# New costs for transposes and a new clock rule in the model that orders a two-layer hybrid encoder

## The chip, the core and the metric

The kernel runs on one core of a Trainium2 chip. The time is the device time of one execution in microseconds. The engines are PE (matmuls; its weight loads are shown as PEld), DVE, ACT and POOL (elementwise work), and SP, which issues DMAs. PE's clock is granted at one of two levels, 1.2 or 2.4 GHz; a granted clock of 1.00 means 2.4 GHz throughout.

## The reference

Two requests (prompt and sample, 1024 tokens of 1024 channels each) go through two layers with shared weights. Cut to what matters:

```
mod = silu(c) @ ada_w + ada_b;  shift, scale, gate = split(mod, 3)
h = rmsnorm(x, norm_pre) * (1 + scale) + shift
u = h @ w_in                  # pool 256 | q 512 | k 128 | v 128 | rg 256 | gate 1024
y = concat(pool_mixer(u_pool), gqa_attention(q, k, v), rglru(u_rg)) * silu(u_gate)
x = x + gate * rmsnorm(y @ w_out, norm_post)
```

The attention has 8 query heads and 2 key/value heads of 64 channels over all 1024 tokens, with normed and rotated q and k. The pool mixer takes centred means with four window lengths. The recurrent branch has a short convolution and a scan in both directions.

## The kernel before

**Slices.** One pair of layer and request is a slice: n = 0 (layer 0, prompt), 1 (layer 0, sample), 2 (layer 1, prompt), 3 (layer 1, sample). Matrix products are made with fp16 operands split in a high and a low part, three matmuls for one. A slice loads x, norms and transposes it (hT), projects and rotates q, k and v, runs the side columns in the order of the list ORDER (recurrent, gate, pool columns), runs 64 attention units, and makes the output projection in 8 tiles of 128 tokens. Slices 0 and 2 also scale and split the weights (wsplit_gen, wo_ahead) and store the split ones for the slices 1 and 3. The second layer's modulation (ada1_gen, weights adaw) is made after the first output projection has begun.

**An attention unit** (L1211 and on) is 128 queries of one head. PE makes 1024 scores in a pair of PSUM banks; DVE takes their maximum (mx); ACT makes the exponential p, then its fp16 part; POOL or DVE subtracts for the low part (both in the tile hh); a transposing DMA (dma_t, L477) turns hh into pT; PE multiplies 24 blocks of pT with v (the PV group).

**The planner.** No loop nest sets the order. Each piece of work is a Python generator with a rank, a *stream*. At each yield it says which engines, tiles, buffers and banks the next step needs. While the program is built, the class Order keeps a simulated time for the engines P, A, D, G (POOL), S (SP's issuing) and X (the transfers), and lets go the stream whose step can go first, and of those that can go now the one with the lowest rank:

```
key = (max(t, self.now), z[0])          # run(): earliest time, then rank
t = max(t, free[e] - tune[e])           # eligible(): look-ahead of engine e
```

The instructions of all engines and SP's queue are written in that order, and engines keep it on the chip. The simulated times come from constants in the helpers (act, tt, mms, dma, dma_t). The clock rule (Order.clock) doubles a matmul's planned time while the simulated PE is not "warm". Some choices, DVE or POOL for a subtraction for example, go to whichever engine the model sees free first (soonest, L481), with a handicap in POOL's favour (slack, hslack, sslack).

**The entries.** TUNE has one dict a slice: ranks of its streams (tab, v, rgt, attn, main, side, w, gate and others; a slice's ranks count from 100 n), look-aheads P, A, D, G, S, X, the number of buffers that are kept free (spare), of score pairs (np) and of output tiles that may be open at once (wopen), the side column from which w_out is loaded (wos), and how side columns are tied to attention units (pace). LAYER has, for a layer, how many modulation weights (fly) and how many pieces of w_out (wfly) may be in flight. These places read the entries that the change touches:

```
wsplit_gen(n, C_K, 256, ("qkv", 0), 100*n + TUNE[n]["q"] if n else START["qw"], keep)   # L1746
sub_any(lo, x, hi, TUNE[0]["hslack"])                                                     # L900
spawn(rank - TUNE[n]["gate"], tail(j, out[0]))                                            # L1372, 1388
cond=lambda: t - left.get("t", 0) < TUNE[n]["wopen"]                                      # L1699
cond=lambda: fly[0] < LAYER[l]["wfly"] and ...                                            # L1586
```

Of the kernel before, what the change touches and what calls it, by code (L numbers as in the profile page):

```python
# [16 lines left out]
P = 128  # L17
D = 1024
# [9 lines left out]


TUNE = [  # L30
    dict(h=-9.8, tab=-61.5, rgw=-62.8, qw=11.3, q=30.3, main=39.6, v=-93.1, rgt=6.2, attn=13.3,
         wprep=16.5, wo=39.7, side=108.5, gate=1.45, ysc=107.7, ysp=100.7, w=68.8, work=8, ds=3, nfly=8,
         s0=4, pace=(4, 61), wos=8, deep=3, f_major=5, spare=0, qkeep=1, wkeep=7, wokeep=0, slack=2.19,
         hslack=1.35, margin=0.33, P=0.6, A=1.22, D=1.01, G=1.25, S=1.3, X=2.5, nb=4, np=2, wopen=3,
         spill=2, sslack=0.0),
    dict(h=-88.0, tab=-138.2, rgw=-45.0, qw=-61.2, q=-181.1, main=65.6, v=-122.9, rgt=21.0, attn=-30.4,
         wprep=107.1, wo=85.3, side=97.8, gate=1.86, ysc=66.7, ysp=108.8, w=79.4, work=8, ds=2, nfly=5,
         s0=0, pace=(14, 64), wos=10, deep=3, f_major=6, spare=2, qkeep=5, wkeep=2, wokeep=9, slack=3.75,
         hslack=3.82, margin=0, P=0.07, A=0.92, D=0.36, G=1.39, S=1.66, X=1.74, nb=4, np=3, wopen=4,
         spill=2, sslack=0.0),  # L40
    dict(h=-56.5, tab=-131.7, rgw=-43.7, qw=-41.0, q=-17.5, main=-3.7, v=-94.1, rgt=51.8, attn=-16.0,
         wprep=71.4, wo=90.7, side=118.4, gate=0.71, ysc=142.5, ysp=110.2, w=62.9, work=6, ds=2, nfly=6,
         s0=3, pace=(15, 38), wos=9, deep=2, f_major=1, spare=4, qkeep=2, wkeep=0, wokeep=1, slack=2.33,
         hslack=2.48, margin=0.36, P=2.36, A=1.02, D=0.83, G=0.625, S=0.35, X=1.72, nb=6, np=2, wopen=4,
         spill=2, sslack=0.0),
    dict(h=-38.8, tab=-7.4, rgw=44.8, qw=-59.1, q=43.0, main=31.5, v=86.0, rgt=62.7, attn=36.1,
         wprep=226.9, wo=-31.1, side=118.1, gate=0.51, ysc=119.3, ysp=81.6, w=59.6, work=10, ds=3, nfly=5,
         s0=5, pace=(0, 64), wos=10, deep=4, f_major=3, spare=1, qkeep=5, wkeep=1, wokeep=0, slack=2.26,
         hslack=2.6, margin=0.87, P=0.28, A=0.14, D=0.45, G=0.9, S=1.99, X=0, nb=4, np=3, wopen=4,
         spill=2, sslack=0.28),  # L50
]
START = dict(x=(6, 16), xr=(-53.8009657012761, 1.4378218455368525), h=11.7, qw=-116.3, qw2=-141.6, qwa=9,
             prt=7, crow=4, prow=2, ada=95.9, keep=0)
LAYER = [
    dict(fly=5, keep=3, wfly=1, wfrom=(0, 0), wrank=15.7, ada=-17.0, akeep=5),
    dict(fly=3, keep=2, wfly=1, wfrom=(1, 1), wrank=163.6, ada=69.7, akeep=8),
]
LAT = {
# [30 lines left out]
class Order:  # L89
# [144 lines left out]
    def clock(self, t):  # L234

        while self.window < int(t / 3.4133):
            self.warm = self.busy / 3.4133 > (0.38 if self.warm else 0.75)
            self.window += 1
            self.busy = 0.0
        return 1.0 if self.warm else 2.0  # L240
# [64 lines left out]
def cols(ap):  # L305
    n = 1
    for x in ap.shape[1:]:
        n *= x
    return n
# [3 lines left out]
def tile_hymba_encoder(  # L313
# [43 lines left out]
    od = Order({"s": NS, "H": 2, "h": NH})  # L357
# [119 lines left out]

    def dma_t(out, in_):
        nc.sync.dma_start_transpose(out=out, in_=in_)
        od.dma(2.3 * cols(in_) / 2048, [out], [in_], 1.7, 0.6)  # L480

    def soonest(*choice):

# [89 lines left out]
    G = {}  # L573
# [522 lines left out]
    def qk_transpose(src, out, key):  # L1096
        yield need("S", [src], s=1)
        t = slot([P, 16, P], F16, "qkT")
        flat = "p a b c d -> p (a b c d)" if len(src.shape) == 5 else "p a b c -> p (a b c)"
        dma_t(t, src.rearrange(flat))  # L1100
        free(src)
        out[key] = t
# [107 lines left out]
    def attn_gen(n, rank):  # L1210
# [3 lines left out]
        def unit(i, S):  # L1214
# [25 lines left out]
            yield need("S", [hh], u=1)  # L1240
            pT = slot([P, 16, P], F16, "pT", "u")
            dma_t(pT, hh.rearrange("p a s -> p (a s)"))
            free(hh)
            if (hp, q) not in O:
# [583 lines left out]
```

## Time and profile before

| what | value |
|---|---|
| median of 3 runs | 1909.93 us (1905.5 to 1915.82) |
| the profiled execution, time | 1907.34 us |
| its span, first to last instruction | 1905.6 us |
| mean granted clock of PE | 0.972 |
| PE busy | 1723.2 us, 90% of the span |
| DVE, ACT, POOL busy | 1292.7, 1136.9, 754.5 us |
| DMA | 323.58 MB, mean 170 GB/s |

Read the table from PE down: what PE does not fill of the span is what an order can change. In the profile, "idle before" is an engine's idle time ahead of a group of instructions, with what ended it, the releaser. L395 is the line of the helper that issues matmuls, so groups are told apart by tiles. Matmul ends are modelled, so a busy PE is not PE at its peak.

### The profile page before, as it was taken

The page shows a single profiled execution, that of the slowest core. Times are in us where ns is not written, and L with a number is a line of the kernel's source. Part 1 is how long each engine was busy: PE and PEld are TensorE (multiplying, and loading weights), DVE is VectorE, ACT ScalarE, POOL GpSimd, SP SyncE. Part 2 cuts the span into 40 slices and gives each one's busy share as a digit, 9 for nine tenths or more (in the row PEclk, how much of TensorE's full clock was granted, in tenths as well). Part 3 has the DMA queues.
Part 4 walks back from the last instruction along what each step waited for, and adds up shares of the span by engine and source line. Part 5 has one row for each costly group of instructions (what it writes and reads, how often), then busy time and mean ns, then how long its engine had stood idle before and what let it go on. Part 6 is the DMA issues. An engine that isn't in the chain of part 4 may idle for free. (4 is left out here: it accounts for less than half of the span.)

```text
span 1905.6 us, 35807 instructions
## 1 busy us (share of the span) xinstructions
PE 1723.2 (90%) x14267; PEld 996.0 (52%) x14267; DVE 1292.7 (68%) x2333; ACT 1136.9 (60%) x1761; POOL 754.5 (40%) x597
## 2 busy tenths in 40 slices
PE   4899898978999888899899999998789999999898
PEld 2564554545455446455456647454445755555543
DVE  4697986776246889677545779867744477867831
ACT  3765766786215666687643277678854256877831
POOL 2722643453321335342524226245553214634423
PEclk9899999998999998999899999999999999999999
DMA  9565799997465667899933365698994322999943
GB/s 342 160 171 166 142 226 236 175 183 232 137 251 166 151 148 133 168 196 217 249 122 122 98 146 112 153 238 163 183 228 171 100 67 37 178 186 195 210 108 130
DMA packets 672592, 323.58 MB, mean 170 GB/s; under 512 B 597880, under 2 KB 628776, under 8 KB 672424
## 3 DMA queue, kind: packets, MB, share of 16 engines
q1 hardware_dynamic: 672424, 321.29, 72.6%
q8 instruction: 111, 1.82, 0.4%
q14 instruction: 57, 0.47, 0.1%
HBM read 128.28 MB, written 46.15 MB: 92 GB/s over the span
## 5 line engine op out<-in xcount | busy, mean ns | idle before, releaser
L423 POOL TENSOR_TENSOR hh<-p,hh 128x1024 f16<-128x1024 f32 x183 | 395.5, 2166 | 425.5 <-ACT hh L410 363.4
L395 PE MATMUL psum<-hT,w 128*128 128x512 f16 x2304 | 538.2, 382 | 8.3 <-ACT w L410 3.4
L459 DVE TENSOR_REDUCE mx<-psum 128x1 f32<-128x1024 f32 x256 | 312.2, 1219 | 128.1 <-PE psum L395 107.1
L395 PEld LDWEIGHTS <-w 128*128 128x128 f16 x2304 | 222.5, 99 | 275.5 <-issue 33.5
L395 PE MATMUL psum<-wo,y 128*128 128x512 f16 x1536 | 345.3, 383 | 4.1 <-DVE y L442 2.3
L395 PE MATMUL psum<-qkT,qkT 128*128 128x512 f16 x1024 | 268.2, 389 | 45.3 <-ACT p L410 26.8
L395 PEld LDWEIGHTS <-pT 128*128 128x128 f16 x6144 | 216.1, 100 | 133.8 <-DMA pT<-hh 96.4
L395 PE MATMUL psum<-v,pT 128*128 128x64 f16 x6144 | 230.3, 196 | 60.7 <-DMA pT<-hh 60.0
L410 ACT ACTIVATE p<-psum,mx,qksc 128x1024 f32<-128x1024 f32 x183 | 219.2, 1199 | 105.0 <-DVE mx L444 60.0
L395 PE MATMUL psum<-w,hT 128*128 128x256 f16 x2304 | 272.1, 275 | 8.6 <-POOL hT L423 8.6
L395 PEld LDWEIGHTS <-hT 128*128 128x128 f16 x2304 | 224.6, 99 | 60.3 <-issue 18.5
L395 PEld LDWEIGHTS <-y 128*128 128x128 f16 x1536 | 150.1, 99 | 179.8 <-issue 7.3
L410 ACT ACTIVATE hh<-p 128x1024 f16<-128x1024 f32 x183 | 192.0, 1053 | 4.0
L395 PEld LDWEIGHTS <-qkT 128*128 128x128 f16 x1024 | 94.7, 100 | 141.9 <-issue 64.0
L410 ACT ACTIVATE junk<-psum 128x512 bf16<-128x512 f32 x64 | 38.3, 598 | 176.5 <-PE psum L395 171.3
L450 DVE SCALAR_TENSOR_TENSOR ot<-psum,ors,gp 128x512 f32<-128x512 f32 x64 | 45.1, 745 | 132.7 <-POOL ors L423 132.7
L423 POOL TENSOR_TENSOR ot<-ot,xres 128x1024 f32<-128x1024 f32 x31 | 72.9, 2352 | 94.0 <-DVE ot L450 58.4
L423 POOL TENSOR_TENSOR ws<-ws,neghalf 128x1 f32<-128x1 f32 x46 | 29.0, 634 | 195.0 <-DVE ws L442 195.0
L423 DVE TENSOR_TENSOR hh<-psum,hh 128x1024 f16<-128x1024 f32 x73 | 89.0, 1219 | 25.2 <-ACT hh L410 24.7
L410 ACT ACTIVATE psum<-psum,mx,qksc 128x1024 f32<-128x1024 f32 x73 | 85.5, 1171 | 28.1 <-DVE mx L444 27.8
L410 ACT ACTIVATE hh<-psum 128x1024 f16<-128x1024 f32 x73 | 74.5, 1020 | 1.7
L410 ACT ACTIVATE gth<-psum,wu 128x512 f32<-128x512 f32 x64 | 43.8, 684 | 44.9 <-PE psum L395 44.9
(212 smaller groups left out, 2100.0 us busy)
## 6 DMA issues: line engine op xcount, KB each, us to landing
adaw<-in_ada_w_dram SPq DMA_DIRECT2D x48, 512.0 KB
wraw<-in_w_in_dram SPq DMA_DIRECT2D x36, 512.0 KB
wd<-w SPq DMA_DIRECT2D x36, 512.0 KB
w<-wd SPq DMA_DIRECT2D x36, 512.0 KB
wo<-wd SPq DMA_DIRECT2D x32, 512.0 KB
woraw<-in_w_out_dram SPq DMA_DIRECT2D x16, 512.0 KB
wd<-wo SPq DMA_DIRECT2D x16, 512.0 KB
xmid<-ot SPq DMA_DIRECT2D x16, 512.0 KB
```

What stands on the lines that cost most here:

```text
L395: nc.tensor.matmul(out[:, :m], lhsT, rhs, start=start and i == 0, stop=stop and i == len(pairs) - 1)
L410: nc.scalar.activation(out=out, in_=in_, func=func, **kw)
L423: eng.tensor_tensor(out=out, in0=a, in1=b, op=op)
L450: nc.vector.scalar_tensor_tensor(out=out, in0=a, scalar=s, in1=b, op0=op0, op1=op1)
L459: nc.vector.tensor_reduce(out=out, in_=a, op=op, **{"axis": AX.X, **kw})
```

## The change

Two constants of dma_t rise: the time that a 2048-column transpose holds the transfer resource, and the time that it holds SP's queue. Both constants of the clock rule change, so that the simulated PE turns warm less readily and stays so a little more readily. Entries of TUNE and LAYER get other values. No instruction is added or removed; the order, and the engine of those operations that have a choice, come out of the planner anew.

```diff
--- before.py
+++ after.py
@@ -28,31 +28,31 @@
 
 
 TUNE = [
-    dict(h=-9.8, tab=-61.5, rgw=-62.8, qw=11.3, q=30.3, main=39.6, v=-93.1, rgt=6.2, attn=13.3,
+    dict(h=-9.8, tab=-61.5, rgw=-62.8, qw=11.3, q=39.5, main=39.6, v=-93.1, rgt=6.2, attn=13.3,
          wprep=16.5, wo=39.7, side=108.5, gate=1.45, ysc=107.7, ysp=100.7, w=68.8, work=8, ds=3, nfly=8,
          s0=4, pace=(4, 61), wos=8, deep=3, f_major=5, spare=0, qkeep=1, wkeep=7, wokeep=0, slack=2.19,
-         hslack=1.35, margin=0.33, P=0.6, A=1.22, D=1.01, G=1.25, S=1.3, X=2.5, nb=4, np=2, wopen=3,
+         hslack=2.0, margin=0.33, P=0.6, A=1.22, D=1.02, G=1.25, S=1.3, X=2.99, nb=4, np=2, wopen=3,
          spill=2, sslack=0.0),
-    dict(h=-88.0, tab=-138.2, rgw=-45.0, qw=-61.2, q=-181.1, main=65.6, v=-122.9, rgt=21.0, attn=-30.4,
+    dict(h=-88.0, tab=-138.2, rgw=-45.0, qw=-61.2, q=-181.1, main=65.6, v=-122.9, rgt=23.6, attn=-14.4,
          wprep=107.1, wo=85.3, side=97.8, gate=1.86, ysc=66.7, ysp=108.8, w=79.4, work=8, ds=2, nfly=5,
-         s0=0, pace=(14, 64), wos=10, deep=3, f_major=6, spare=2, qkeep=5, wkeep=2, wokeep=9, slack=3.75,
-         hslack=3.82, margin=0, P=0.07, A=0.92, D=0.36, G=1.39, S=1.66, X=1.74, nb=4, np=3, wopen=4,
+         s0=0, pace=(14, 64), wos=10, deep=3, f_major=6, spare=1, qkeep=5, wkeep=2, wokeep=9, slack=3.75,
+         hslack=3.82, margin=0, P=0.07, A=1.29, D=0.36, G=1.39, S=1.66, X=1.74, nb=4, np=3, wopen=4,
          spill=2, sslack=0.0),
-    dict(h=-56.5, tab=-131.7, rgw=-43.7, qw=-41.0, q=-17.5, main=-3.7, v=-94.1, rgt=51.8, attn=-16.0,
-         wprep=71.4, wo=90.7, side=118.4, gate=0.71, ysc=142.5, ysp=110.2, w=62.9, work=6, ds=2, nfly=6,
+    dict(h=-56.5, tab=-120.9, rgw=-43.7, qw=-41.0, q=-17.5, main=-3.7, v=-95.2, rgt=51.8, attn=-16.0,
+         wprep=71.4, wo=90.7, side=118.4, gate=0.1, ysc=142.5, ysp=110.2, w=62.9, work=6, ds=2, nfly=6,
          s0=3, pace=(15, 38), wos=9, deep=2, f_major=1, spare=4, qkeep=2, wkeep=0, wokeep=1, slack=2.33,
-         hslack=2.48, margin=0.36, P=2.36, A=1.02, D=0.83, G=0.625, S=0.35, X=1.72, nb=6, np=2, wopen=4,
-         spill=2, sslack=0.0),
+         hslack=2.48, margin=0.36, P=2.36, A=1.02, D=0.83, G=0.625, S=0.35, X=1.72, nb=6, np=2, wopen=3,
+         spill=2, sslack=0),
     dict(h=-38.8, tab=-7.4, rgw=44.8, qw=-59.1, q=43.0, main=31.5, v=86.0, rgt=62.7, attn=36.1,
-         wprep=226.9, wo=-31.1, side=118.1, gate=0.51, ysc=119.3, ysp=81.6, w=59.6, work=10, ds=3, nfly=5,
-         s0=5, pace=(0, 64), wos=10, deep=4, f_major=3, spare=1, qkeep=5, wkeep=1, wokeep=0, slack=2.26,
-         hslack=2.6, margin=0.87, P=0.28, A=0.14, D=0.45, G=0.9, S=1.99, X=0, nb=4, np=3, wopen=4,
+         wprep=226.9, wo=-31.1, side=118.1, gate=0.51, ysc=119.3, ysp=81.6, w=57.1, work=10, ds=3, nfly=5,
+         s0=5, pace=(0, 64), wos=9, deep=4, f_major=3, spare=1, qkeep=5, wkeep=1, wokeep=0, slack=2.26,
+         hslack=2.98, margin=0.87, P=0.28, A=0.15, D=0.45, G=0.9, S=1.99, X=0, nb=4, np=3, wopen=4,
          spill=2, sslack=0.28),
 ]
 START = dict(x=(6, 16), xr=(-53.8009657012761, 1.4378218455368525), h=11.7, qw=-116.3, qw2=-141.6, qwa=9,
              prt=7, crow=4, prow=2, ada=95.9, keep=0)
 LAYER = [
-    dict(fly=5, keep=3, wfly=1, wfrom=(0, 0), wrank=15.7, ada=-17.0, akeep=5),
+    dict(fly=6, keep=3, wfly=4, wfrom=(0, 0), wrank=15.7, ada=-17.0, akeep=5),
     dict(fly=3, keep=2, wfly=1, wfrom=(1, 1), wrank=163.6, ada=69.7, akeep=8),
 ]
 LAT = {
@@ -234,7 +234,7 @@
     def clock(self, t):
 
         while self.window < int(t / 3.4133):
-            self.warm = self.busy / 3.4133 > (0.38 if self.warm else 0.75)
+            self.warm = self.busy / 3.4133 > (0.37 if self.warm else 0.8)
             self.window += 1
             self.busy = 0.0
         return 1.0 if self.warm else 2.0
@@ -477,7 +477,7 @@
 
     def dma_t(out, in_):
         nc.sync.dma_start_transpose(out=out, in_=in_)
-        od.dma(2.3 * cols(in_) / 2048, [out], [in_], 1.7, 0.6)
+        od.dma(2.55 * cols(in_) / 2048, [out], [in_], 1.8, 0.6)
 
     def soonest(*choice):
```

## Rows read from the trace of the kernel before

**Rows 1.** The page: span, instructions, and section 1 (busy us of each engine).

```profile
span 1905.6 us, 35807 instructions
...
PE 1723.2 (90%) x14267; PEld 996.0 (52%) x14267; DVE 1292.7 (68%) x2333; ACT 1136.9 (60%) x1761; POOL 754.5 (40%) x597
```

**Rows 2.** Busy time by stage; columns in the first line.

```profile
core 0: us, PE busy (x) PEld busy (x) DVE busy (x) ACT busy (x) POOL busy (x), PEclk, DMA share, GB/s
0.00:100.00 100.00, 66.61 (x433) 43.85 (x434) 57.92 (x192) 54.64 (x96) 46.99 (x63) 0.91 0.75 252
100.00:208.00 108.00, 105.31 (x633) 62.39 (x632) 92.52 (x185) 62.22 (x91) 29.17 (x25) 1.00 0.52 155
208.00:435.00 227.00, 192.56 (x2167) 113.06 (x2164) 173.71 (x298) 170.49 (x253) 115.67 (x65) 0.96 1.05 200
435.00:645.00 210.00, 204.27 (x1206) 111.19 (x1207) 116.88 (x259) 85.43 (x151) 57.95 (x75) 0.97 0.55 185
645.00:925.00 280.00, 244.19 (x2478) 142.99 (x2476) 215.29 (x327) 189.68 (x279) 112.99 (x63) 0.95 0.92 176
925.00:1110.00 185.00, 178.12 (x1011) 102.95 (x1012) 108.57 (x233) 86.27 (x155) 58.08 (x75) 0.97 0.44 141
1110.00:1405.00 295.00, 259.10 (x2547) 150.15 (x2544) 226.03 (x368) 216.66 (x308) 143.35 (x80) 0.98 0.85 169
1405.00:1600.00 195.00, 190.99 (x1111) 110.83 (x1111) 111.70 (x189) 87.57 (x152) 59.04 (x68) 1.00 0.35 115
1600.00:1835.00 235.00, 219.46 (x2403) 130.29 (x2401) 174.60 (x265) 172.89 (x249) 106.96 (x55) 0.99 0.98 178
1835.00:1905.60 70.60, 62.59 (x292) 28.32 (x290) 15.45 (x21) 11.00 (x32) 24.30 (x31) 0.96 0.32 112
```

**Rows 3.** Groups of PE matmuls, whole span: busy, mean ns, idle before, releasers.

```profile
L395 PE MATMUL psum<-wo,y 128*128 128x512 f16 x1536 | 345.3, 383 | 4.1 <-DVE y L442 2.3 <-DVE sg L450 0.8 <-DVE hT L423 0.5
...
L395 PE MATMUL psum<-w,hT 128*128 128x256 f16 x2304 | 272.1, 275 | 8.6 <-POOL hT L423 8.6
L395 PE MATMUL psum<-qkT,qkT 128*128 128x512 f16 x1024 | 268.2, 389 | 45.3 <-ACT p L410 26.8 <-DVE hh L423 8.0 <-DVE rt L467 6.2
L395 PE MATMUL psum<-v,pT 128*128 128x64 f16 x6144 | 230.3, 196 | 60.7 <-DMA pT<-hh 60.0
```

**Rows 4.** Who waited for whom: us in total, times, longest us.

```profile
PEld L395 <- DMA pT<-hh: 96.4, 90, 3.9
...
PE psum L395 <- DMA pT<-hh: 60.0, 59, 3.5
```

**Rows 5.** Timeline, 1355 to 1366: start us, us, idle before.

```profile
1359.96 1.02 PE L395 MATMUL psum<-qkT,qkT 128*128 128x512 f16 x4 [1.45 <-ACT p L410]
...
1363.13 1.02 PE L395 MATMUL psum<-qkT,qkT 128*128 128x512 f16 x4 [1.45 <-ACT p L410]
```

**Rows 6.** Timeline of SP's DMA queue, 400 to 440: start us, us.

```profile
399.86 30.63 SPq L479 DMA_TRANSPOSE pT<-hh  x11
```

**Rows 7.** Waits of SP's DMA queue: us in total, times, longest us.

```profile
SPq L479 <- POOL hh L423: 271.4, 118, 39.4
```

**Rows 8.** Tile hT in 0 to 100: ns min/median/max, first and last start.

```profile
L423 POOL TENSOR_TENSOR hT<-xT,hT x16: 1148/1152/1995, 45.6 to 76.5; 128x512 f16<-128x512 f32 x16
```

**Rows 9.** Tile adaw in 400 to 700, same columns.

```profile
L395 PE MATMUL psum<-adaw,scol x96: 592/592/617, 539.7 to 600.4; 128*32 128x512 f32 x96
```

**Rows 10.** Tile qkT in 480 to 1000, same columns.

```profile
L395 PE MATMUL psum<-qkT,qkT x256: 376/379/634, 633.2 to 907.0; 128*128 128x512 f16 x128
```

**Rows 11.** Tile woraw in 0 to 450, same columns.

```profile
L471 SPq DMA_DIRECT2D woraw<-in_w_out_dram x8: 383/404/1383, 69.6 to 240.6; - x8
L410 ACT ACTIVATE junk<-woraw x8: 1040/1052/1057, 76.5 to 246.5; 128x1024 bf16<-128x1024 f32 x8
```

**Rows 12.** Busy time in two stretches of the third attention stage.

```profile
1300.00:1350.00 50.00, 39.06 (x457) 23.04 (x456) 42.46 (x55) 40.20 (x56) 25.76 (x15) 0.93 0.97 181
1350.00:1400.00 50.00, 36.15 (x512) 22.43 (x511) 32.28 (x44) 42.04 (x56) 36.71 (x19) 1.00 1.02 183
```

## The prediction

> **What bounds the kernel now.** I read the page first. PE is busy for 1723.2 of 1905.6 us, no other engine for more than 68% [rows 1], so the span is PE's work plus 182.4 us in which PE is idle. The change adds and removes no matmul. It can win only idle time, and time in which PE works at the lower of its two clocks.
>
> The second view cuts the span into stages, and the reader should subtract PE's busy time from the length of each [rows 2]. The four attention stages are idle for 34.4, 35.8, 35.9 and 15.5 us (15, 13, 12 and 7% of their length), the start for 33.4, the three stages between attention stages for 5.7, 6.9 and 4.0, the rest for 10.7. So three of the four attention stages hold 106 us, and the fourth shows what another order of the same operations reaches. The column PEclk says how much of each stage ran at 1.2 instead of 2.4 GHz: (1 - PEclk) times the length, summed over the stages, is 55 us, an upper limit of what the lower clock cost. It is concentrated where PE is idle (14 us in 645 to 925, 9 in each of 0 to 100 and 208 to 435; none in 1405 to 1600), so it follows the waits.
>
> The third view says what ended PE's idle time [rows 3]. Before the matmuls that read pT it waited 60.7 us, 60.0 of them for the transfer that transposes hh into pT; before the score matmuls 45.3 us, for ACT, DVE hh and DVE rt. The list of waits counts 59 of the first kind, none over 3.5 us [rows 4]. The score waits are of another sort: in the third attention stage the same gap of 1.45 us comes back each 3.17 us [rows 5], each time until ACT has read a score pair out of PSUM. How many pairs may be open (np) is not touched.
>
> Two rows of SP's queue tell of the transposes. In a dense stretch 11 were issued in 30.63 us, 2.78 us each [rows 6]. And transposes at the head of that queue waited 271.4 us for POOL's hh [rows 7]; each load or store behind them waits too.
>
> **The change, part by part.** All of it acts on the planner; the chip runs the same operations in another order, some on another engine.
>
> *Transposes, 2.3 to 2.55 us on the transfer resource, 1.7 to 1.8 on the issuing queue.* Against 2.78 in the trace the model was short by 0.48 us a transpose and is now short by 0.23: half of the error goes. A PV group that the old model placed when its pT "is there" met a pT that wasn't. With 64 transposes a slice, the planned finish moves by up to 64 x 0.25 = 16 us per slice, so each later choice moves too. What this is worth has no row of its own. From below: the waits for pT may shrink by the half of the error that goes, 60 x 0.25 / 0.48 = 31 us won. From above: an order can also come out worse. The attention stages differ by 35.9 - 15.5 = 20.4 us under one model, so I allow a loss of 20. I take a third of the 60 us, 20 us won, nearer to the gain because the error corrected is the one PE is seen to wait for.
>
> The Trainium skill, "DMA: Bandwidth & Descriptors", section "Latency and other measured facts", gives a DMA transpose 261 GB/s; a 512 KB tile would then take 2.0 us (an estimate), the old constant would already be too high, and this term would be nothing. The row's 2.78 us disagrees, and I go by the row.
>
> *The clock rule.* The planner's PE now gets back to full speed less readily. That changes only planned times after bubbles. If the idle time of three attention stages falls by 20 of 106 us, their 29 us of clock loss [rows 2] should fall by the same fifth: 5 us. Bounds: nothing, and twice that.
>
> *Entries that cannot matter.* The q of slice 0 is read for later slices only; hslack is read from slice 0's entry alone, so that of slice 3 is dead; sslack 0.0 to 0 is one value. Slice 0's hslack rises from 1.35 to 2.0, which favours POOL in the 16 first-slice subtractions, but POOL already has all 16 [rows 8]. A rank decides only among streams that can go at the same moment. For rgt (121.0 to 123.6), v (105.9 to 104.8), gate (317.7 to 318.3) and slice 3's w (359.6 to 357.1), as absolute ranks, no other stream lies between old and new. Slice 1's attention units (69.1 to 85.1) and slice 2's tables (68.3 to 79.1) pass the second layer's modulation at 69.7 and the first output projection at 68.8; that modulation's matmuls end at 600.4 [rows 9] and slice 1's first score matmul starts at 633.2 [rows 10]. Nothing is left to pass. All of these: 0. What covers them is that the rivals have finished; were the modulation 33 us later, its weight loads would stand among slice 1's transposes.
>
> *The split of w_out, wfly 1 to 4.* Today the eight pieces go one at a time, loads from 69.6 to 240.6 [rows 11]. With four in flight the last two loads and up to three stores leave the first attention stage, which begins at 208. The start moved 252 GB/s [rows 2], so 512 KB takes 2.1 us: at most 5 x 2.1 = 10 us won, if each stood before a wanted transpose. Against that, three pieces come forward past the input, weight and modulation loads on SP's queue: 3 x 2.1 us of transfer and 3 x 1.05 us of ACT's squares, at most 9 us lost while PE still waits for its first operands; the splits on DVE and POOL behind them go along. DVE is 86% busy from 100 to 208, yet PE idles for only 2.7 us there, so I take 0. fly 5 to 6 lets one 512 KB load go earlier: 0, bound 2.
>
> *The other live entries.* wopen 4 to 3 in slice 2: slice 0 has 3 already and its projection stage idles 5.7 us against slice 1's 6.9 with 4 [rows 2], so 0, bound 2. spare 2 to 1 lets slice 1 take buffers earlier in a stage that idles 5.7: bound 5.7 won. X (2.5 to 2.99), D (1.01 to 1.02), A (0.92 to 1.29; 0.14 to 0.15) and wos 10 to 9 shift the moment at which an operation or a load is let go by half a microsecond or one column: no price of their own, inside the 20 above.
>
> *What comes late next.* A PV group that no longer waits lets PE reach the next score pair sooner, and that waits for ACT or DVE. Today's 41 us of such waits stay, and I charge a third of the 25 us won to them: 8 us back.
>
> Sum: -20 - 5 + 8 = -17 us.
>
> **The rivals.**
>
> *A. The waits only move: no change.* PSUM pairs and ACT's reads bind the score waits [rows 5]; the order is drawn anew and the idle time stays near 182 us. For it: the time lies in many waits of a microsecond or two, and most edited entries are dead. Against: the fourth attention stage, with half the others' idle share. Time: 1910 as before, or 1905 if the clock's 5 us are won alone.
>
> The Trainium skill, "TensorE: Matmul & The Clock Gate", section "What's actually happening", says of the same side that the ramp costs a typical kernel under 1% of its span and that a model should not be fitted to its details; by that rule the new clock rule buys nothing, which is this rival. The trace leaves room for more: its bound of 55 us is 2.9%.
>
> *B. Fillers run out: slower.* In an attention stage the columns of the gate projections fill PE between units. If the planner, expecting slower transposes, spends them early, the last units run bare, as in 1300 to 1400, where PE worked for 75.2 of 100 us while ACT was at 82% [rows 12]. If the fourth stage ended like that, its 15.5 us of idle time would become 35.9, +20.4, and its clock loss about 3 more: 1933. It decides from the point at which PE's busy share over the last 100 us of that stage falls below 85%. Against: pace keeps its values there and ties units to columns.
>
> **How the numbers follow.** The profiled execution took 1907.3 us (span 1905.6 and 1.7 around it), 2.6 below the median. 1907.3 - 17 = 1890.3, plus 2.6 is 1893. A measurement here tells about 0.5% from no change, 9.5 us: faster means below 1900.4, slower above 1919.5. Chances: my forecast 0.52 (its own range: 31 + 10 won, 6 in the small entries, none given back, 1863; at the other end 1900), rival A 0.26, rival B 0.22. The range runs from 1866 to 1933: it leaves out little of the lower end and that part of B in which more than one stage is bare.
>
> **What would show it.** Right: the waits for pT fall from 60 towards 40 us, the first three attention stages idle for less than 95 us together, woraw loads end before 200 us, POOL's 16 hT subtractions stay. Wrong: pT waits as before (the model's error was not what PE waits for), score waits that grow by what pT waits lose (A), or a last 100 us of any attention stage below 85% on PE (B). A start stage that idles for over 40 us would say that wfly's early pieces cost what I set at nothing.

## The result, and the profile after

The changed kernel takes 1878.99 us (median of 4 runs, 1876.88 to 1881.69), the kernel before beside it 1908.3: a ratio of 0.984, 95% interval 0.981 to 0.987. That is 29 us, 1.6%. The forecast was 17 us won, 47 at most by its own sum (1863 us), and the range held the time. The sum was too small and, as the experiments show, most of its terms were not what made it.

The page of the changed kernel, the same two lines as [rows 1]:

```profile
span 1875.1 us, 35819 instructions
...
PE 1712.4 (91%) x14267; PEld 990.7 (53%) x14267; DVE 1280.2 (68%) x2327; ACT 1140.2 (61%) x1767; POOL 760.5 (41%) x602
```

The matmuls are the same 14267. PE's idle time fell from 182.4 to 162.7 us, and its busy time by 10.8 us for the same work. So the 30.5 us between the two profiled executions are 19.7 of idle time and 10.8 of busy time. That split is of one execution each. In the profile of a_spare below, which runs the same operations in the same order, PE idles for 156.2 us and is busy for 1721.8, so the sum of the two is firmer than either part.

The stages, cut at the same events as in [rows 2]; columns in the first line:

```profile
core 0: us, PE busy (x) PEld busy (x) DVE busy (x) ACT busy (x) POOL busy (x), PEclk, DMA share, GB/s
0.00:100.00 100.00, 63.98 (x389) 41.87 (x390) 60.05 (x189) 55.29 (x100) 48.85 (x65) 0.80 0.79 270
100.00:203.00 103.00, 101.55 (x538) 52.86 (x536) 84.34 (x191) 65.13 (x92) 22.47 (x22) 1.00 0.53 157
203.00:442.00 239.00, 211.65 (x2317) 127.41 (x2315) 195.96 (x315) 178.43 (x264) 117.87 (x69) 0.98 1.02 197
442.00:637.00 195.00, 191.96 (x1190) 106.35 (x1190) 104.52 (x243) 80.73 (x145) 51.81 (x65) 1.00 0.56 182
637.00:910.00 273.00, 244.70 (x2502) 143.85 (x2501) 205.19 (x329) 199.12 (x288) 112.03 (x66) 0.96 0.95 187
910.00:1086.00 176.00, 170.37 (x993) 100.18 (x992) 103.30 (x228) 78.78 (x146) 54.34 (x73) 0.98 0.45 141
1086.00:1376.00 290.00, 256.94 (x2550) 149.33 (x2548) 230.75 (x369) 209.03 (x301) 151.55 (x82) 0.99 0.87 171
1376.00:1574.00 198.00, 191.80 (x1108) 111.04 (x1109) 109.05 (x187) 91.01 (x157) 59.15 (x70) 0.99 0.35 114
1574.00:1799.00 225.00, 211.28 (x2375) 126.81 (x2373) 171.57 (x262) 171.71 (x248) 118.04 (x60) 1.00 1.01 186
1799.00:1875.10 76.10, 68.13 (x318) 30.98 (x316) 15.46 (x21) 11.00 (x32) 24.40 (x31) 0.98 0.30 104
```

Subtract again. The first three attention stages idle for 27.4, 28.3 and 33.1 us, 88.7 together instead of 106; the fourth for 13.7 instead of 15.5. The three stages between hold 14.9 instead of 16.6. Only the start is worse: 36.0 us idle instead of 33.4, at a granted clock of 0.80 instead of 0.91. The mean granted clock rose from 0.972 to 0.975, so the upper limit of what the lower clock costs fell from 53.4 to 46.9 us (1 minus the clock, times the span). Two executions do not show a rise, though: the four runs after lie at 0.971 to 0.975, the 53 runs of the kernel before that stand beside the experiments at 0.961 to 0.974.

PE's groups that answer to [rows 3], and the waits that answer to [rows 4]:

```profile
L395 PE MATMUL psum<-qkT,qkT 128*128 128x512 f16 x1024 | 265.7, 385 | 39.3 <-ACT p L410 24.7 <-DVE rt L467 7.3 <-DVE ru L423 4.7
...
L395 PE MATMUL psum<-v,pT 128*128 128x64 f16 x6144 | 225.8, 194 | 54.8 <-DMA pT<-hh 54.6
```

```profile
PEld L395 <- DMA pT<-hh: 85.1, 77, 4.5
...
PE psum L395 <- DMA pT<-hh: 54.6, 49, 4.3
```

The waits for pT fell from 60.0 to 54.6 us (47.8 in a_spare), not to the 40 that the forecast named. The score waits fell too, from 45.3 to 39.3, where the forecast had them grow.

Where along the span the time was won is read best from the first and the last score matmul of a slice (tile qkT; ns min/median/max, first and last start). Of the kernel before, the third and fourth slice, which stand beside [rows 10] for the second:

```profile
L395 PE MATMUL psum<-qkT,qkT x256: 376/379/634, 1110.5 to 1390.4; 128*128 128x512 f16 x128
```

```profile
L395 PE MATMUL psum<-qkT,qkT x256: 376/379/380, 1592.2 to 1818.1; 128*128 128x512 f16 x128
```

Of the changed kernel, the second, third and fourth slice:

```profile
L395 PE MATMUL psum<-qkT,qkT x256: 376/379/634, 626.8 to 888.4; 128*128 128x512 f16 x128
```

```profile
L395 PE MATMUL psum<-qkT,qkT x256: 376/379/634, 1086.7 to 1362.0; 128*128 128x512 f16 x128
```

```profile
L395 PE MATMUL psum<-qkT,qkT x256: 376/379/380, 1566.0 to 1777.7; 128*128 128x512 f16 x128
```

In these two executions the changed kernel is 6.4 us ahead when the second slice's scores begin, 23.8 at the third's, 26.2 at the fourth's and 30.5 at the end. More than half, 17.4 us, is won between the second slice's first score and the third's.

The two rows that answer to [rows 8] and [rows 11], tiles hT and woraw:

```profile
L423 POOL TENSOR_TENSOR hT<-xT,hT x16: 1147/1158/2142, 47.9 to 80.6; 128x512 f16<-128x512 f32 x16
```

```profile
L471 SPq DMA_DIRECT2D woraw<-in_w_out_dram x8: 382/408/1278, 71.5 to 96.4; - x8
```

POOL has the same 16 subtractions, and the eight pieces of w_out are now loaded between 71.5 and 96.4.

The last 100 us of the first, the third and the fourth attention stage after, columns as above:

```profile
342.00:442.00 100.00, 81.73 (x965) 46.72 (x963) 80.44 (x113) 80.95 (x118) 57.30 (x33) 0.97 1.07 200
1276.00:1376.00 100.00, 82.70 (x1014) 48.96 (x1012) 70.96 (x95) 73.74 (x101) 59.98 (x30) 0.98 1.03 187
1699.00:1799.00 100.00, 92.22 (x1051) 52.70 (x1049) 74.04 (x101) 72.67 (x105) 45.10 (x22) 1.00 1.03 199
```

The fourth stage does not run bare: PE works 92 of 100 us. The first and the third fall below the mark that I had set, 85% in any attention stage. It was a poor one, since the kernel before fell below it in the same two stages already:

```profile
335.00:435.00 100.00, 84.44 (x1036) 51.60 (x1033) 72.23 (x108) 77.78 (x114) 50.56 (x26) 0.94 1.04 184
1305.00:1405.00 100.00, 75.21 (x967) 45.35 (x965) 71.04 (x92) 77.27 (x104) 60.33 (x32) 0.97 1.03 186
```

### The profile page after: what moved, and what is told of

It reads as the page before. It is cut to its first block, busy times and chain, and to the rows that moved or that the text cites. A ratio compares the mean times of both kernels' runs of the same rounds, so it can differ in the third digit from the quotient of the medians.

```text
span 1875.1 us, 35819 instructions
## 1 busy us (share of the span) xinstructions
PE 1712.4 (91%) x14267; PEld 990.7 (53%) x14267; DVE 1280.2 (68%) x2327; ACT 1140.2 (61%) x1767; POOL 760.5 (41%) x602
## 4 chain that ended last, share of the span: by engine, by line
PE 32%; DVE 11%; issue 5%; ACT 4%; DMA 4%; POOL 4%; SPq 1%; POOLq 0%; ACTq 0%; DVEq 0%
PE psum L395 31%; POOL hh L423 4%; DMA pT<-hh 3%; DVE mx L459 3%; ACT p L410 2%; DVE psum L423 1%; ACT hh L410 1%; PE psum L403 1%; DVE y L450 1%; DMA xt<-xmid 1%; DVE sq L423 1%; SPq L479 1%; DVE hh L423 1%; DVE pdf L450 0%; DVE qss L459 0%
## 5 line engine op out<-in xcount | busy, mean ns | idle before, releaser
L423 POOL TENSOR_TENSOR hh<-p,hh 128x1024 f16<-128x1024 f32 x187 | 406.8, 2179 | 416.2 <-ACT hh L410 382.2
L395 PE MATMUL psum<-qkT,qkT 128*128 128x512 f16 x1024 | 265.7, 385 | 39.3 <-ACT p L410 24.7
L410 ACT ACTIVATE p<-psum,mx,qksc 128x1024 f32<-128x1024 f32 x187 | 224.1, 1199 | 106.8 <-DVE mx L444 63.9
L395 PE MATMUL psum<-v,pT 128*128 128x64 f16 x6144 | 225.8, 194 | 54.8 <-DMA pT<-hh 54.6
L410 ACT ACTIVATE hh<-p 128x1024 f16<-128x1024 f32 x187 | 196.5, 1053 | 4.9
L423 DVE TENSOR_TENSOR hh<-psum,hh 128x1024 f16<-128x1024 f32 x69 | 84.1, 1218 | 31.7 <-ACT hh L410 31.5
L410 ACT ACTIVATE psum<-psum,mx,qksc 128x1024 f32<-128x1024 f32 x69 | 80.8, 1170 | 24.1 <-DVE mx L444 19.4
L410 ACT ACTIVATE hh<-psum 128x1024 f16<-128x1024 f32 x69 | 70.3, 1019 | 1.7
L423 POOL TENSOR_TENSOR qrs<-qrs,neghalf 128x8 f32<-128x8 f32 (+1 forms) x48 | 68.7, 1432 | 4.0
```

The source lines that it names most:

```text
L395: nc.tensor.matmul(out[:, :m], lhsT, rhs, start=start and i == 0, stop=stop and i == len(pairs) - 1)
L410: nc.scalar.activation(out=out, in_=in_, func=func, **kw)
L423: eng.tensor_tensor(out=out, in0=a, in1=b, op=op)
```

## The experiments

Three theories were on trial. **M**: the corrected cost of a transpose in the model makes the gain. **E** (later **P**): the entries make it, each by what it does. **L**: any live edit makes the planner draw another order, orders spread by about 1%, and the change is a well selected draw.

First, the instruction lists that the planner writes. The changed kernel with all of the entries that the prediction called dead put back to their old values (q, both hslack, sslack, rgt, attn, tab, v, gate, slice 3's w) has the same lists on all engines. (attn and tab are dead as a pair: with attn alone put back the units' rank, 69.1, would pass the tables' new 79.1, and the lists change.) fly alone, put back, changes nothing either, and neither does slice 3's A. Live are seven entries (X, D, spare, slice 1's A, wopen, wos, wfly) and the two model edits. Of these nine each was undone alone below, but for wos, which has no run.

**Both model edits alone (b_model).**

```diff
 kernel before, entries as before
-            self.warm = self.busy / 3.4133 > (0.38 if self.warm else 0.75)
+            self.warm = self.busy / 3.4133 > (0.37 if self.warm else 0.8)
-        od.dma(2.3 * cols(in_) / 2048, [out], [in_], 1.7, 0.6)
+        od.dma(2.55 * cols(in_) / 2048, [out], [in_], 1.8, 0.6)
```

> The kernel before with the two model edits alone (transposes 2.55 and 1.8, clock rule), all entries as before. Theory M (the transposes' cost in the model is what makes the gain): PE's waits for pT fall from 60 us towards 45, time at or below 1893 us. Theory E (the entries make it): 1900 to 1920, as the entries were picked for the old constants. Theory L (any redraw of the order lands anywhere within about 1%, and the change is one good draw): 1890 to 1930, with no link between the time and the waits for pT.

Measured: 1915.8 us, ratio 1.004 (1.003 to 1.005): slower. PE's PV group:

```profile
L395 PE MATMUL psum<-v,pT 128*128 128x64 f16 x6144 | 233.9, 197 | 70.9 <-DMA pT<-hh 66.6 <-ACT p L410 3.3
```

The waits for pT did not fall: they are 66.6 us against 60.0, a difference no larger than that between two profiles of one order (54.6 in the changed kernel, 47.8 in a_spare). Theory M falls in its plain form: the better constants, by themselves, won nothing, not even in the wait they are about.

**The entries alone (b_tune).**

```diff
 kernel before, model edits left out
-TUNE, LAYER as before
+TUNE, LAYER as after
```

> The kernel before with the new entries alone, old transposes' cost and old clock rule. Theory M: near 1908 us, waits for pT stay near 60 us. Theory E: most of the gain, below 1890. Theory L: 1890 to 1930.

Measured: 1904.2 us, ratio 0.997 (0.996 to 0.999), 4 us of the 29. Theory E falls too.

**The changed kernel with the old cost of a transpose (a_nodma).**

```diff
-        od.dma(2.55 * cols(in_) / 2048, [out], [in_], 1.8, 0.6)
+        od.dma(2.3 * cols(in_) / 2048, [out], [in_], 1.7, 0.6)
```

> The changed kernel with the old cost of a transpose (2.3 and 1.7). Theory M: waits for pT grow from 54.6 us to 60 or more and 10 us or more of the 30 us gain go. Theory E: under 1885. Theory L: 1885 to 1925, without an order to it.

Measured: 1920.8 us, ratio to the kernel before 1.007 (1.005 to 1.010). The page:

```profile
span 1920.2 us, 35852 instructions
...
PE 1734.1 (90%) x14267; PEld 999.4 (52%) x14267; DVE 1283.9 (67%) x2332; ACT 1143.2 (60%) x1766; POOL 752.2 (39%) x597
```

42 us go, more than the change won, while the waits for pT are 55.2 us, as in the changed kernel. Idle time is up by 23.4 us and busy time by 21.7. Of theory M's two marks the loss of time came, and the longer waits did not.

**The changed kernel with the old clock rule (a_noclk).**

```diff
-            self.warm = self.busy / 3.4133 > (0.37 if self.warm else 0.8)
+            self.warm = self.busy / 3.4133 > (0.38 if self.warm else 0.75)
```

> The changed kernel with the old clock rule. My prediction gave that edit 5 of 25 us: 1884 by theory M and E. Theory L: a redrawn order, 1885 to 1925, so a loss of more than 10 us speaks for L, since the rule changes planned times only after bubbles.

Measured: 1914.6 us, ratio 1.004 (1.003 to 1.006). PE's PV group:

```profile
L395 PE MATMUL psum<-v,pT 128*128 128x64 f16 x6144 | 230.6, 196 | 41.1 <-DMA pT<-hh 40.8
```

The waits for pT are 14 us shorter than in the changed kernel (7 us shorter than in a_spare), and the time is 36 us longer. The loss of far more than 10 us speaks for L, and the row says that the waits for pT do not tell the time of an order.

**One hundredth of a microsecond (a_D).**

```diff
 TUNE[0] of the changed kernel
-D=1.02
+D=1.01
```

> The changed kernel with one entry back, slice 0's look-ahead of DVE from 1.02 to 1.01 us. By itself 0.01 us is worth nothing on the chip; it only makes the planner draw another order, from the first 2 per cent of PE's instructions on. Theory L (the gain is one selected draw out of orders that spread by about 1%): 1890 to 1920. Theory P (the parts carry the gain and small shifts do not matter): 1875 to 1885.

Measured: 1903.8 us, ratio to the kernel before 0.998 (0.996 to 0.999). The page, and the PV group:

```profile
span 1902.1 us, 35851 instructions
...
PE 1730.3 (91%) x14267; PEld 1000.8 (53%) x14267; DVE 1281.4 (67%) x2334; ACT 1141.9 (60%) x1761; POOL 762.8 (40%) x602
```

```profile
L395 PE MATMUL psum<-v,pT 128*128 128x64 f16 x6144 | 229.9, 196 | 34.1 <-DMA pT<-hh 33.8
```

This is the test that decides. An edit that can mean nothing to the chip costs 25 of the 29 us, by redrawing the order from the first 2% of PE's instructions. The waits for pT fall to 33.8 us, the lowest of all kernels here, and the kernel is slower all the same. The loss comes bit by bit; the third slice's scores begin 13.0 us later than in the changed kernel, and the end is 27.0 later:

```profile
L395 PE MATMUL psum<-qkT,qkT x256: 376/379/631, 1099.7 to 1381.8; 128*128 128x512 f16 x128
```

**One piece of w_out in flight (a_wfly).**

```diff
 LAYER[0] of the changed kernel
-wfly=4
+wfly=1
```

> The changed kernel with one piece of w_out in flight in layer 0 instead of four. My prediction set this edit at 0, with 10 us to either side: 1869 to 1889 by theory P. Theory L: 1890 to 1920, with idle time and time at the lower clock spread over all slices, the last two too, which hold no split of layer 0.

Measured: 1886.1 us, ratio 0.989 (0.987 to 0.991): 7 us of the 29 go. That lies in theory P's range and 4 us below theory L's. The loads spread out again, and the stages 0 to 100 and 203 to 442 read:

```profile
L471 SPq DMA_DIRECT2D woraw<-in_w_out_dram x8: 377/423/423, 71.9 to 261.1; - x8
```

```profile
0.00:100.00 100.00, 65.89 (x402) 42.26 (x403) 58.32 (x188) 50.81 (x90) 48.03 (x63) 0.86 0.73 247
203.00:442.00 239.00, 211.44 (x2280) 125.82 (x2278) 192.48 (x329) 181.56 (x266) 105.40 (x59) 0.96 1.05 204
```

The start idles for 34.1 us at a clock of 0.86, against 36.0 at 0.80 with four in flight. That is no cost of the early pieces that could be told: a_spare and a_wopen, which have four in flight too, idle there for 36.9 and 34.3 us. The first attention stage idles for 27.6 us against 27.4: the loads that left it won nothing there that shows. The 7 us are not lost in these stages at all. When the fourth slice's scores begin, the two kernels are 1.1 us apart; when they end, 8.0:

```profile
L395 PE MATMUL psum<-qkT,qkT x256: 376/379/635, 1567.1 to 1785.7; 128*128 128x512 f16 x128
```

That slice holds no split of layer 0, so the loss fits a redrawn order and not the split's place.

**wopen back in slice 2 (a_wopen).**

```diff
 TUNE[2] of the changed kernel
-wopen=3
+wopen=4
```

> The changed kernel with slice 2's wopen back from 3 to 4. The order is the same up to slice 2's output projection (73% of PE's instructions). My prediction: at most 2 us either way, 1877 to 1881. Theory L: the gain of the first three slices stays, the rest is drawn anew: 1875 to 1895.

Measured: 1882.6 us, ratio 0.987 (0.985 to 0.989). The median is 3.6 us above that of the changed kernel, but the runs overlap (1880.8 to 1884.3 and 1876.9 to 1881.7), so a loss is not shown. In the profile the third slice's scores begin at 1092.3 instead of 1086.7, at the end of a stretch in which the order is the same:

```profile
L395 PE MATMUL psum<-qkT,qkT x256: 375/379/634, 1092.3 to 1367.9; 128*128 128x512 f16 x128
```

So single executions of one order differ by 5.6 us there.

**spare back in slice 1 (a_spare).**

```diff
 TUNE[1] of the changed kernel
-spare=1
+spare=2
```

> The changed kernel with slice 1's spare back from 1 to 2. The order differs in one stretch (some 4% of PE's instructions around slice 0's output projection and slice 1's start) and is the same behind it. My prediction: up to 5.7 us won by the edit, so 1879 to 1885. Theory L, a small redraw: 1875 to 1890.

Measured: 1880.1 us, ratio 0.985 (0.984 to 0.987): no difference from the changed kernel that can be told. The 4% of PE's instructions differ in the buffers that they name; by operation, tile and shape the lists of all engines are those of the changed kernel, in the same order. So this run says little of a redraw, but its profile is a second look at the same order:

```profile
span 1878.0 us, 35819 instructions
...
PE 1721.8 (92%) x14267; PEld 997.4 (53%) x14267; DVE 1279.5 (68%) x2327; ACT 1140.1 (61%) x1767; POOL 760.7 (41%) x602
```

```profile
L395 PE MATMUL psum<-v,pT 128*128 128x64 f16 x6144 | 229.3, 196 | 48.1 <-DMA pT<-hh 47.8
```

The spans are 2.9 us apart, but PE is busy for 9.4 us more, idles for 6.5 less and waits 6.8 less for pT. Differences of that size in one of these columns say nothing of an order.

**X back in slice 0 (a_X), A back in slice 1 (a_A).**

```diff
 a_X: TUNE[0] of the changed kernel
-X=2.99
+X=2.5
 a_A: TUNE[1] of the changed kernel
-A=1.29
+A=0.92
```

> The changed kernel with slice 0's look-ahead of transfers back from 2.99 to 2.5 us; the order differs from the first instructions on. Theory P: within 1875 to 1889. Theory L: 1885 to 1920; the four variants measured so far whose order differs from the start lie at 1886 to 1921, mean 1906.

> The changed kernel with slice 1's look-ahead of ACT back from 1.29 to 0.92 us; the first 21% of PE's instructions keep their order. Theory P: within 1875 to 1889. Theory L: 1885 to 1915.

Measured: 1910.3 us, ratio 1.000 (0.999 to 1.002), and 1908.2, ratio 1.000 (0.998 to 1.001). Each of the two takes the whole gain away. Neither was given a price in the prediction. Whether an entry does this by its own effect or by the redraw alone, one run of each cannot tell.

**The kernel before, redrawn (b_D, b_wfly).**

```diff
 b_D: TUNE[0] of the kernel before
-D=1.01
+D=1.02
 b_wfly: LAYER[0] of the kernel before
-fly=5, wfly=1
+fly=6, wfly=4
```

> The kernel before with slice 0's look-ahead of DVE at 1.02 instead of 1.01 us and nothing else. Theory L: the kernel before is itself a selected order of the old model, so a redraw is likelier slower than 1909 than faster: 1900 to 1930. Theory P: 1904 to 1914, no change.

> The kernel before with four pieces of w_out of layer 0 in flight instead of one (and fly 6). If having the pieces early is worth something by itself, as in the changed kernel, where undoing it cost 7 us, 1900 to 1905. Theory L: 1900 to 1930, and the shorter list of transfers in the first attention stage shows in that stage alone.

Measured: 1925.0 us, ratio 1.008 (1.006 to 1.010), and 1930.7, ratio 1.010 (1.008 to 1.012). Against the kernel before beside them (1910.0 us) both shifts cost time, 15 and 21 us, the second just beyond theory L's 1930. That fits a kernel before that was a selected draw itself; two shifts do not prove it. In b_wfly the pieces are loaded early, and the same two stages as above read:

```profile
L471 SPq DMA_DIRECT2D woraw<-in_w_out_dram x8: 369/404/739, 69.8 to 94.8; - x8
```

```profile
0.00:100.00 100.00, 59.50 (x385) 40.64 (x386) 56.48 (x181) 58.22 (x102) 48.37 (x65) 0.86 0.82 273
203.00:442.00 239.00, 209.80 (x2307) 126.65 (x2306) 182.50 (x308) 176.60 (x259) 122.73 (x68) 0.96 1.00 192
```

Here the start idles for 40.5 us instead of 33.4, which is the sign that the prediction had named for a cost of the early pieces. But nothing of it is left when the third slice's scores begin, at 1107.3, 3.2 us ahead of the kernel before. The loss comes behind that, where nothing of layer 0 is split: these scores last from 1107.3 to 1413.1, 306 us instead of 280.

```profile
L395 PE MATMUL psum<-qkT,qkT x256: 376/379/634, 1107.3 to 1413.1; 128*128 128x512 f16 x128
```

**All of them side by side.** Span, idle time (span less PE's busy time), mean granted clock and the PV group's idle time are of the profiled executions. The median of the kernel before is that of the runs beside the changed kernel; beside the experiments it was 1908.7 to 1910.0:

| kernel | median us | span | PE idle | PE busy | clock | idle before PV |
|---|---|---|---|---|---|---|
| before | 1908.3 | 1905.6 | 182.4 | 1723.2 | 0.972 | 60.7 |
| after | 1879.0 | 1875.1 | 162.7 | 1712.4 | 0.975 | 54.8 |
| b_model | 1915.8 | 1912.2 | 187.1 | 1725.1 | 0.964 | 70.9 |
| b_tune | 1904.2 | 1903.2 | 175.8 | 1727.4 | 0.962 | 65.2 |
| a_nodma | 1920.8 | 1920.2 | 186.1 | 1734.1 | 0.961 | 55.9 |
| a_noclk | 1914.6 | 1910.6 | 180.8 | 1729.8 | 0.963 | 41.1 |
| a_D | 1903.8 | 1902.1 | 171.8 | 1730.3 | 0.967 | 34.1 |
| a_wfly | 1886.1 | 1882.9 | 159.9 | 1723.0 | 0.973 | 42.4 |
| a_wopen | 1882.6 | 1882.5 | 158.8 | 1723.7 | 0.967 | 51.6 |
| a_spare | 1880.1 | 1878.0 | 156.2 | 1721.8 | 0.971 | 48.1 |
| a_X | 1910.3 | 1905.2 | 177.9 | 1727.3 | 0.958 | 53.8 |
| a_A | 1908.2 | 1908.1 | 181.4 | 1726.7 | 0.971 | 51.9 |
| b_D | 1925.0 | 1924.1 | 191.3 | 1732.8 | 0.965 | 73.1 |
| b_wfly | 1930.7 | 1930.0 | 197.4 | 1732.6 | 0.965 | 60.2 |

Read the columns against the span. All of PE's idle time together goes with it over the 14 kernels (156 to 163 us in the four fastest, 191 and 197 in the two slowest). PE's busy time varies by 22 us for equal work, and is lowest in the profile with the highest clock; 9 us of the 22 lie between after and a_spare, which are one order. The last column tells little: 34.1 in a kernel of 1904 us, 54.8 in the fastest.

## Why the prediction was right, and where its steps failed

**The bound held.** Idle time and time at the lower clock were all there was to win, and 19.7 and 10.8 us of them make the 30.5 in the two profiles. Three attention stages gave 17.4 of the idle time, as the stage view had suggested.

**The step that failed is the first term**, 20 us for transposes that are costed better. The waits for pT gave 5.4 of 60.0 us, 12.2 by the profile of a_spare. And the link that the term rests on, from a better cost through fewer waits to a shorter time, is refuted by a_D and a_noclk, where these waits are 33.8 and 40.8 us and the time is 25 and 36 us longer, and by b_model, where the better costs alone did not shorten them. What the runs showed in its place: the gain is a property of the order as a whole, and a shift of 0.01 us takes 25 of its 29 us away. That the forecast's direction and range held is therefore luck as far as this term goes.

The term's premise was weak too. Its 2.78 us are the mean of one dense stretch of SP's queue. Over all 256 transposes of pT in the kernel before, the queue took from 1.63 to 6.85 us for one (ns min/median/max):

```profile
L479 SPq DMA_TRANSPOSE pT<-hh x256: 1627/2410/6853, 201.2 to 1825.3; - x128
```

By their median, 2.41 us, the old 2.3 was 0.11 us short and the new 2.55 is 0.14 too long; by their mean, 2.64 us, the two are 0.34 and 0.09 short. So that half of an error goes is not shown, and one constant cannot stand for so wide a spread.

**The live entries were mis-sized.** "No price of their own, inside the 20 above" was wrong for X, D and slice 1's A: undoing one costs 31, 25 and 29 us. Each redraws everything behind it, and a redraw can cost more than the 20 us allowed. For D, by 0.01 us, the redraw is all there is; for X and A a price of their own is not excluded.

**The clock's term** was 5 us with bounds of 0 and 10. PE's busy time fell by 10.8 us between the two profiles, at the upper bound, and the limit of the clock's loss by 6.5; but by the profile of a_spare, the same order, the busy time fell by 1.4. So no run shows what this term was worth. That any of it stems from the new rule is not shown: undoing the rule costs 36 us, as any redraw may.

**The 8 us given back** to score waits did not come; they fell by 6.0. In a_D they are below those of before as well (40.8 us). One order can shorten several kinds of wait at once, so charging one for the other had no ground in these runs.

**The small terms held in the changed kernel.** The dead entries are exactly dead. wfly at 0 with 10 to either side: undone 7 us in the changed kernel, lost in its last slice; in the kernel before the same edit cost 21 us, outside the bound, all of it behind the third slice's first score. spare and wopen: medians 1.1 and 3.6 us apart, neither clear of the spread of the runs.

**The rivals.** A, no change, did not come to pass for the change, but it describes b_tune, a_D, a_X and a_A, the changed kernel with a part missing. B, bare last units in the fourth stage, did not happen; PE fell below its mark of 85% in two other stages, before as after. The sign that was set against A, the fourth stage's low idle share, was the right one to weigh: orders do differ by tens of us.

**What the gain is, then.** The undone parts do not add up: b_model loses 7 us and b_tune wins 4, together they win 29, and five of the eight single removals take most of it or all. Against redraws from the first quarter of the order on (a_D, a_wfly, a_X, a_A: 1886 to 1910, mean 1902) the changed kernel is 23 us ahead; the kernel before, at 1910 us beside them, is 18 ahead of its two (mean 1928). Both look like selected orders. That the new model and entries also moved the whole neighbourhood, from 1928 to 1902, is what these means suggest. It stays open: it rests on two and four draws that spread by 6 and 24 us, and two further draws contradict it, b_model with the new model at 1916 and b_tune with the old one at 1904. How either order was found is not on record. What in the faster order makes it faster is open too, since no single kind of wait goes with the time.

## What to carry to other kernels

Where a planner writes the order, first find by building which entries change the instruction lists at all; here 12 of the 19 changed entries did nothing. Then run a few orders that differ by a meaningless shift before giving any gain a cause: here such shifts moved the time by 15 and 25 us, so a single order says little of the edit that led to it. Add up PE's idle time and its lower clock over the whole span, and not one kind of wait, since the most visible wait went down in orders that were slower. And profile one order twice before splitting a gain into its parts: here idle and busy time moved by 7 and 9 us without a change of order.

## What the runs showed of the hardware that had not been expected

The same 14267 matmuls kept PE busy for 1712.4 to 1734.1 us. Part of that is not the order's doing: one order, in the changed kernel and in a_spare, gave 1712.4 and 1721.8 us, with mean granted clocks of 0.975 and 0.971, and the clock of the kernel before ran from 0.961 to 0.974 over its 53 runs. Yet the medians of the granted clock over all runs of a kernel go with the time: 0.959 to 0.966 in the six slowest orders (1910 us and more), 0.970 to 0.973 in the four fastest. In the profiles of the six PE is busy for 1725.1 us or longer, in those of the four for at most 1723.7. So the slow orders had more idle time and also more work at 1.2 GHz, as a rule and not without exception: the kernel before, at 1908 to 1910 us, has medians of 0.968 to 0.971.
